# Second block's attention scores: the keys' low parts stored once per half, or twice, one below the other

## The chip, the cores and the metric

One NeuronCore of one Trainium2 chip runs the whole program. The metric is device time in microseconds (us) of that core. Engines are named as in the profile: PE (TensorE, matmuls), PEld (its weight loads), DVE (VectorE), ACT (ScalarE), POOL (GpSimd), SP (SyncE, which issues most DMAs).

## The reference

A transformer in float32 for 512 tokens of width 1024. A first block (hybrid mixer and a mixture of 32 experts) is followed by a second block of two equal layers. Each layer of the second block does, in short:

```python
h = rms_norm_2(x, norm_g); proj = h @ w_in          # split into q, k, v, z, gates
# stick-breaking attention, 8 heads of 64: scores, then a product of (1 - sigmoid) from the right
z = einsum('bhqd,bhkd->bhqk', qb, kb) * 64**-0.5    # by query blocks of 128, keys 0..end
o_a = w(z) @ vb
# sparse attention (nsa): 8 query heads share 2 key heads; compressed keys, selected keys, a window
ss = einsum('bgrqd,bgqkd->bgrqk', qb, ks) * scale   # selected: with 512 tokens all blocks up to the query
sw = einsum('bgrqd,bgkd->bgrqk', qb, kw) * scale    # window of 512
x = x + (sigmoid(ga)*(y_a @ w_up_a) + sigmoid(gb)*(y_b @ w_up_b)) @ w_out
```

Products of matrices are to be accurate to float32, so the kernel splits each operand into a high part (rounded to fp32r, the type that PE multiplies fast) and a low part, the rest, and adds the products that matter.

## The kernel before, in words

**Products.** A projection runs three matmuls for each of eight 128-row chunks: high x high, low x high, high x low (`rows_mm`, L371 to L373, 256 columns; `cols_mm`, L396 to L398, 512 columns). Each matmul has its own weight load, also where two in a row have the same stationary operand (L371 and L372).

**Scores.** A head has 64 channels, so the two parts of a query fill the 128 rows of one operand: `q_stack` (L405) puts the high part of head h in its 64 rows and the low part in the other 64. `k_stack` (L421) makes `kh`, which has the high part of the keys in both halves, with two ACT copies from PSUM (L428) and two DVE copies from SBUF (L434), and writes the low part once, to the head's own 64 rows of `kl` (DVE, L430). One `kl` tile holds the low parts of the two `k_stack` calls that belong together. `qk` (L437) then makes one score tile of 128 queries by 128, 256, 384 or 512 keys with two matmuls into the same PSUM bank: L442 over 128 rows gives (high + low query) x high key, and L443 over 64 rows gives high query x low key.

**Where scores are used.** `stick_attention` (L1713) calls `qk` 32 times a layer, four for each head. `nsa_weights` (L1976) calls it 64 times a layer: four query blocks, two key groups, two branches, four heads. That is 192 calls over the two layers, 48 of each width. The stick weights go through ACT (tanh, L1728), DVE (L1732, L1733), a scan along the keys (L1737) into one of two buffers `sbs`, and a subtraction that reads the scan (L1739). The nsa weights go through a mask and a maximum on DVE (L459, L461), an exponential on ACT (L464), and DVE again.

**Order.** Within a layer `weave` (L1651) mixes strands of work by estimated costs: the first part of the stick attention with the projections of its second half; the rest of it with the nsa projections and the compression network (`compress`); the nsa attention (L1949) with the large gate and up projections. The framework then places the instructions on the engines, and its order on each engine is fixed in the program: each engine runs its own list in order and waits where an operand or a buffer isn't ready.

**Buffers.** Most tiles of the second block, of up to 4 KB a partition, come from one pool, `hd`, of `NHD` = 17; a new tile waits until one is free. Smaller ones come from `P` (11). `sbs` has two buffers, the table of `gain_tables` (`rtab`, used by `rope_tile`) has one of its own, and so has `nf`, in which `nsa_finish` (L2021) makes the final sum.

Of the kernel before, what the change touches and what calls it, by code (L numbers as in the profile page):

```python
# [13 lines left out]
F32R = mybir.dt.float32r  # L14
I32 = mybir.dt.int32
BF16 = mybir.dt.bfloat16
AF = mybir.ActivationFunctionType
OP = mybir.AluOpType
AXX = mybir.AxisListType.X

P = 128
S = 512
NT = S // P
# [57 lines left out]
def rev(ap):  # L81
    a = [list(x) for x in ap.ap]
    s, n = a[-1]
    return bass.AP(tensor=ap.tensor, offset=ap.offset + s * (n - 1), ap=a[:-1] + [[-s, n]])


class Kern:
# [9 lines left out]


    NW, NWS = 2, 3
    KACT = False  # L100

    def run(self):
        with self.early():
            self.consts()
            with self.phase("first", NW2=1, NHT=17, NHD=8, NP=8):
                x = self.first_mixer()
            with self.phase("moe", NW2=4, NP=1):
                x, aT, late = self.moe(x)
        with self.phase("second", NW2=0, NHD=17, NP=11):
            self.second_block(x, aT, late)  # L110

    def early(self):
# [305 lines left out]
                                               op0=OP.mult, op1=OP.subtract)  # L418
        return q

    def k_stack(self, pt, kl):  # L421


        nc = self.nc
        kh = self.t([P, 2, S], F32R, tag="hd", bufs=self.NHD)
        rows = (slice(0, 64), slice(64, 128))
        for h in range(2):
            nc.scalar.activation(kh[rows[h], h, :], pt[rows[h], :], AF.Copy)  # L428
        for h in range(2):
            nc.vector.tensor_tensor(kl[rows[h], :], pt[rows[h], :], kh[rows[h], h, :], op=OP.subtract)  # L430
            if self.KACT:
                nc.scalar.copy(kh[rows[1 - h], h, :], kh[rows[h], h, :])
            else:
                nc.vector.tensor_copy(kh[rows[1 - h], h, :], kh[rows[h], h, :])  # L434
        return kh

    def qk(self, q, h, ts, k, n, out):  # L437

        nc = self.nc
        kh, kl = k  # L440
        r = slice(64 * h, 64 * h + 64)
        nc.tensor.matmul(out[:, :n], q[:, h, ts], kh[:, h, :n], start=True, stop=False)  # L442
        nc.tensor.matmul(out[:, :n], q[r, h, ts], kl[r, :n], start=False, stop=True)  # L443

    def transpose_rows(self, rows, f0, out, scale=None):

# [1176 lines left out]
    def gain_tables(self, gains):  # L1623

        nc = self.nc
        out = self.t([P, len(gains), 4, NT, 32], tag="rtab", bufs=1)
        for b, g in enumerate(gains):
            for n, (tab, half) in enumerate(((self.cos, 0), (self.sin, 1), (self.cos, 1), (self.sin, 0))):
                nc.gpsimd.tensor_tensor(out[:, b, n], tab, g[:, None, 32 * half:32 * half + 32].to_broadcast([P, NT, 32]),
                                        op=OP.mult)  # L1630
        return out
# [59 lines left out]

    def stick_qkz(self, l, aT, n, out):
        nc, W = self.nc, self.A["w_in_2"]
        kl = []

        def cons_q(m, ps):
            out[0, m] = self.q_stack(ps, 64 ** -0.5)

        def cons_k(m, ps):
            if not m:  # L1700
                kl.append(self.t([P, 2, S], F32R, tag="hd", bufs=self.NHD))
            out[2, m] = self.k_stack(ps, kl[0][:, m, :]), kl[0][:, m, :]

        def cons_z(m, ps):
            if not m:
                out[6] = self.hd_pair()
            o = out[6][:, m, :]
            nc.scalar.activation(o, ps, AF.Tanh, scale=0.5)
            nc.vector.scalar_tensor_tensor(o, o, 1.0, ps, op0=OP.add, op1=OP.mult)
        for base, cons in ((0, cons_q), (2, cons_k), (6, cons_z)):  # L1710
            yield from self.cols_steps(aT, W[l, base + n], cons)

    def stick_attention(self, qkz, v, y):  # L1713

        nc = self.nc

        def weights(h):

            c = h // 2
            q, k = (qkz[c // 2][base, c % 2] for base in (0, 2))  # L1720
            big, small = self.t([P, 1024], tag="hd", bufs=self.NHD), self.t([P, S], tag="P", bufs=self.NP)
            ws = [big[:, 896:1024], small[:, 0:256], big[:, 512:896], big[:, 0:512]]
            for i, w in enumerate(ws):
                n_ = (i + 1) * P
                sp = self.psum("s")
                self.qk(q, h % 2, slice(i * P, (i + 1) * P), k, n_, sp)
                f = self.t([P, S], tag="P", bufs=self.NP)
                nc.scalar.activation(f[:, :n_], sp[:, :n_], AF.Tanh, scale=0.5)  # L1728
                if i in self.SACT:
                    nc.scalar.activation(f[:, :n_], f[:, :n_], AF.Copy, scale=-0.5, bias=0.5)  # L1730
                else:
                    nc.vector.tensor_scalar(f[:, :n_], f[:, :n_], -0.5, 0.5, op0=OP.mult, op1=OP.add)  # L1732
                nc.vector.tensor_tensor(f[:, n_ - P:n_], f[:, n_ - P:n_], self.C["smask"], op=OP.max)  # L1733
                self.sbr = 1 - self.sbr
                sc = self.sbs[self.sbr]
                o = S - n_
                nc.vector.tensor_tensor_scan(rev(sc[:, o:S]), rev(f[:, :n_]),  # L1737
                                             self.zero.to_broadcast([P, n_]), 1.0, op0=OP.mult, op1=OP.add)
                nc.vector.tensor_tensor(w, sc[:, o + 1:], sc[:, o:S], op=OP.subtract)  # L1739
            return ws  # L1740

        ws = weights(0)
        yield 2.1
        for h in range(8):
            nxt = weights(h + 1) if h < 7 else None
            yield 2.1
            if h % 2 == 0:
                po = self.psum("o")
            r = slice(64 * (h % 2), 64 * (h % 2) + 64)
            for j in range(NT):  # L1750
                pt = self.psum("tr")
                for i in range(j, NT):
                    nc.tensor.transpose(pt[:, i * P:(i + 1) * P], ws[i][:, j * P:(j + 1) * P], self.ident)
                wT = self.t([P, S], tag="P", bufs=self.NP)
                nc.scalar.copy(wT[:, j * P:], pt[:, j * P:])
                nc.tensor.matmul(po[r, j * P:], v[h // 4][:, j, (h % 4) * 64:(h % 4 + 1) * 64], wT[:, j * P:],
                                 start=(j == 0), stop=(j == NT - 1), skip_group_check=True)
            ws = nxt
            if h % 2:
                c = h // 2  # L1760
                f = self.t([P, S], tag="P", bufs=self.NP)
                nc.vector.scalar_tensor_tensor(f, qkz[c // 2][6][:, c % 2, :], 0.5, po, op0=OP.mult, op1=OP.mult)
                nc.scalar.activation(y[0][:, c, :], f, AF.Copy)
                nc.vector.tensor_tensor(y[1][:, c, :], f, y[0][:, c, :], op=OP.subtract)
            yield 3.2
# [126 lines left out]
    def nsa_projections(self, l, aT, N):  # L1892
        nc, A, W = self.nc, self.A, self.A["w_in_2"]
# [11 lines left out]
                N["q"].append(self.q_stack(pt))  # L1905

        def k_stacks(rows):
            kl = self.t([P, 2, S], F32R, tag="hd", bufs=self.NHD)
            for n in range(2):
                pt = self.psum("tr")  # L1910
                self.transposes(rows, n * P, pt)
                N["k"].append((self.k_stack(pt, kl[:, n, :]), kl[:, n, :]))

        N["k"], N["q"] = [], []
        late = None
        for src, gains, dst in ((11, gk, k_stacks), (8, [gq], q_stacks), (9, None, q_stacks)):
            r = self.hd()
# [9 lines left out]
        v = N["v"] = [self.t([P, 2, 4, 2, 64], F32R, tag="hd", bufs=self.NHD) for _ in range(2)]  # L1927
# [93 lines left out]
    def nsa_finish(self, N, i, g, po):  # L2021

        nc = self.nc
        ts = slice(i * P, (i + 1) * P)
        cs = slice(2 * g, 2 * g + 2)
        f = self.t([P, 2, P], tag="nf", bufs=1)
        p4 = po.rearrange("p (c m q) -> p m c q", c=2, m=2)
        u = self.t([P, 2, 2, P], tag="P", bufs=self.NP)
        nc.scalar.copy(u[64:128], p4[64:128])
        for m in range(2):  # L2030
            nc.vector.tensor_tensor(f[64 * m:64 * m + 64], p4[0:64, m], u[64:128, m], op=OP.add)
        nc.vector.scalar_tensor_tensor(f, f, 0.5, N["z"][g][:, :, ts], op0=OP.mult, op1=OP.mult)
        if "y" not in N:
            N["y"] = self.split_y()
        yh, yl = N["y"]
        self.split(f, yh[:, cs, ts], yl[:, cs, ts])
# [131 lines left out]
    def second_block(self, x0, hl, late):  # L2168
        nc = self.nc
# [3 lines left out]
        self.fold = self.t([P, 64], tag="fold", bufs=1)  # L2173
        nc.vector.tensor_tensor(self.fold, self.ident[:, 0:64], self.ident[:, 64:128], op=OP.add)

        self.sbs, self.sbr = [self.t([P, S + 1], tag=f"sbs{n}", bufs=1) for n in range(2)], 0
        for sc in self.sbs:
            nc.vector.memset(sc[:, S:], 1.0)
        self.rope_tables()
        xo = self.O["out"].rearrange("(t p) d -> t p d", p=P)  # L2180
        x1 = self.x_in_dram(1)
# [147 lines left out]
```

## Time and profile before

| what | value |
|---|---|
| time, median of 3 runs | 2686.78 us (2685.45 to 2688.61) |
| the profiled execution's own time | 2686.94 us |
| its span (first to last instruction) | 2685.1 us |
| PE busy | 2561.9 us (95%) |
| DVE busy | 1796.4 us (67%) |
| ACT busy | 1275.6 us (48%) |

Busy shares are averages over stages with different limits: a stage is read from the windows. Matmuls overlap in the records (one may start before the one before it has ended), so what a matmul takes from PE is read from the distance between the starts of neighbours, not from its duration. The second block runs from about 1640 us to the end; its second layer repeats the first some 548 us later.

### The profile page before, as it was taken

The page shows a single profiled execution, that of the slowest core. Times are in us where ns is not written, and L with a number is a line of the kernel's source. Part 1 is how long each engine was busy: PE and PEld are TensorE (multiplying, and loading weights), DVE is VectorE, ACT ScalarE, POOL GpSimd, SP SyncE. Part 2 cuts the span into 40 slices and gives each one's busy share as a digit, 9 for nine tenths or more (in the row PEclk, how much of TensorE's full clock was granted, in tenths as well). Part 3 has the DMA queues.
Part 4 walks back from the last instruction along what each step waited for, and adds up shares of the span by engine and source line. Part 5 has one row for each costly group of instructions (what it writes and reads, how often), then busy time and mean ns, then how long its engine had stood idle before and what let it go on. Part 6 is the DMA issues. An engine that isn't in the chain of part 4 may idle for free.

```text
span 2685.1 us, 40235 instructions
## 1 busy us (share of the span) xinstructions
PE 2561.9 (95%) x15431; PEld 2003.9 (75%) x15431; DVE 1796.4 (67%) x3400; ACT 1275.6 (48%) x2202; POOL 159.9 (6%) x151
## 2 busy tenths in 40 slices
PE   5998879999999999999999969989999999999998
PEld 5875678777777778777777757776777887767778
DVE  6886667666666688666666645596775656877764
ACT  3443546545555566444455534444444433534443
POOL 1001010100000000000000010011001000100001
PEclk9998788999999999999999989999999999999999
DMA  7531236999699999999999952221112521311124
GB/s 283 203 120 65 77 134 254 367 376 367 228 359 376 380 363 344 383 379 376 380 376 384 378 192 79 67 93 66 46 48 79 189 95 49 111 63 48 33 84 151
DMA packets 85828, 566.77 MB, mean 211 GB/s; under 512 B 9984, under 2 KB 10576, under 8 KB 22144
## 3 DMA queue, kind: packets, MB, share of 16 engines
q1 hardware_dynamic: 76368, 536.55, 51.5%
q0 software_dynamic: 7968, 24.16, 3.9%
q10 hardware_dynamic: 1296, 3.44, 0.3%
q8 instruction: 123, 2.02, 0.3%
q14 instruction: 73, 0.60, 0.1%
HBM read 543.93 MB, written 20.19 MB: 210 GB/s over the span
## 4 chain that ended last, share of the span: by engine, by line
PE 72%; DVE 6%; DMA 2%; ACT 2%; issue 2%; POOL 1%; ACTq 0%; DVEq 0%; SPq 0%; POOLq 0%
PE mm L396 5%; PE mm L397 5%; PE mm L398 5%; PE mm L1290 4%; PE s L1290 4%; PE o L1290 4%; PE o L1278 3%; PE mm L1276 3%; PE mm L1278 2%; PE o L1276 2%; PE o L1277 2%; PE s L1276 2%; PE mm L1277 2%; PE s L1278 2%; PE s L1277 2%; PE o L1192 2%
## 5 line engine op out<-in xcount | busy, mean ns | idle before, releaser
L1260 ACT ACTIVATE wh<-w 128x1024 fp32r<-128x1024 f32 x324 | 337.5, 1060 | 286.2 <-DMA w<-w_exp 131.7
L1261 DVE TENSOR_TENSOR wl<-w,wh 128x1024 fp32r<-128x1024 f32 x324 | 388.2, 1221 | 84.8 <-ACT wh L1260 84.0
L215 DVE TENSOR_TENSOR wl<-w,wh 128x1024 fp32r<-128x1024 f32 x194 | 237.0, 1223 | 176.3 <-ACT wh L214 175.1
L214 ACT ACTIVATE wh<-w 128x1024 fp32r<-128x1024 f32 x194 | 204.8, 1059 | 234.6 <-PE mm L397 97.9
L372 PE MATMUL mm<-wl,aTh 128*128 128x256 f32 x816 | 238.1, 293 | 5.6 <-DVE wl L215 5.6
L371 PE MATMUL mm<-wh,aTh 128*128 128x256 f32 x816 | 238.7, 294 | 2.2 <-ACT wh L214 1.3
L373 PE MATMUL mm<-wh,aTl 128*128 128x256 f32 x816 | 238.1, 293 | 0.8 <-DVE aTl L309 0.8
L396 PE MATMUL mm<-aTh,wh 128*128 128x512 f32 x560 | 228.3, 408 | 0.0
L397 PE MATMUL mm<-aTl,wh 128*128 128x512 f32 x560 | 225.5, 403 | 0.0
L398 PE MATMUL mm<-aTh,wl 128*128 128x512 f32 x560 | 224.9, 402 | 0.0
L372 PEld LDWEIGHTS mm<-wl,aTh 128*128 128x128 f32 x816 | 161.0, 197 | 9.4 <-DVE wl L215 6.3
L371 PEld LDWEIGHTS mm<-wh,aTh 128*128 128x128 f32 x816 | 160.4, 197 | 6.6 <-ACT wh L214 1.9
L373 PEld LDWEIGHTS mm<-wh,aTl 128*128 128x128 f32 x816 | 160.7, 197 | 4.5 <-issue 3.1
L464 ACT ACTIVATE P<-s,smx 128x256 f32<-128x256 f32 (+3 forms) x176 | 92.7, 528 | 86.8 <-DVE smx L461 85.7
L1261 DVE TENSOR_TENSOR spl<-w,sph 128x1024 fp32r<-128x1024 f32 x108 | 132.1, 1223 | 1.2 <-ACT sph L1260 1.2
L1260 ACT ACTIVATE sph<-w 128x1024 fp32r<-128x1024 f32 x108 | 114.2, 1057 | 26.5 <-PE mm L1277 10.3
L396 PEld LDWEIGHTS mm<-aTh,wh 128*128 128x128 f32 x560 | 106.3, 190 | 24.1 <-issue 4.9
L398 PEld LDWEIGHTS mm<-aTh,wl 128*128 128x128 f32 x560 | 106.3, 190 | 23.8 <-issue 3.0
L397 PEld LDWEIGHTS mm<-aTl,wh 128*128 128x128 f32 x560 | 105.8, 189 | 23.2 <-issue 3.8
L1319 DVE TENSOR_SCALAR eg<-s 128x512 f32<-128x512 f32 (+1 forms) x66 | 37.6, 569 | 111.6 <-PE s L1280 71.6
L1290 PE MATMUL mm<-w,xN 128*64 128x256 f32 x960 | 110.2, 382 | 0.0
L1290 PE MATMUL s<-w,xN 128*64 128x256 f32 x960 | 109.5, 381 | 0.0
(617 smaller groups left out, 6073.7 us busy)
## 6 DMA issues: line engine op xcount, KB each, us to landing
w<-w_exp SPq DMA_DIRECT2D x384, 1024.0 KB, 8.9
w<-w_in SPq DMA_DIRECT2D x57, 1024.0 KB, 4.8
w<-w_out SPq DMA_DIRECT2D x24, 1024.0 KB, 4.9
w<-ada_w SPq DMA_DIRECT2D x19, 1024.0 KB, 4.9
w<-cmp_w SPq DMA_DIRECT2D x8, 1024.0 KB, 4.8
w<-w_up SPq DMA_DIRECT2D x16, 512.0 KB, 3.3
xm<-hd POOLq DMA_DIRECT2D x5, 512.0 KB, 3.6
aTl<-ada_w SPq DMA_DIRECT2D x2, 1024.0 KB, 7.8
```

Of the source, the lines that this page charges most:

```text
L214: self.nc.scalar.activation(hi, src, AF.Copy)
L215: (self.nc.gpsimd if pool else self.nc.vector).tensor_tensor(lo, src, hi, op=OP.subtract)
L371: nc.tensor.matmul(v[:, q, :], ah[k][:, ts], w_h, start=(k == 0), stop=False)
L372: nc.tensor.matmul(v[:, q, :], ah[k][:, ts], w_l, start=False, stop=False)
L373: nc.tensor.matmul(v[:, q, :], al[k][:, ts], w_h, start=False, stop=(k == kk - 1))
L396: nc.tensor.matmul(ps, w_h, ah[k], start=(k == 0), stop=False)
L397: nc.tensor.matmul(ps, w_h, al[k], start=False, stop=False)
L398: nc.tensor.matmul(ps, w_l, ah[k], start=False, stop=(k == kk - 1))
L1260: nc.scalar.activation(hi, w, AF.Copy)
L1261: (nc.gpsimd if n in self.LO_POOL else nc.vector).tensor_tensor(lo, w, hi, op=OP.subtract)
L1276: nc.tensor.matmul(ps, xh[:, k, :], wh[:, q, :], start=(k == 0), stop=False)
L1290: nc.tensor.matmul(ps[CN * c:CN * (c + 1), 0:256], a, w[:, c * 256:(c + 1) * 256], start=(n == 0), stop=(n == len(jobs) - 1))
```

## The change

The low parts get the form of the high parts. `k_stack` now allocates a `kl` tile of its own, of the size of `kh`, and writes the low part of each head to both halves, so that `qk` runs both matmuls over 128 rows with the same stationary operand; the product low query x low key is added to the score by that. All copies of the high part are now made by ACT from PSUM, and all four low parts by DVE from PSUM.

```diff
-        with self.phase("second", NW2=0, NHD=17, NP=11):
+        with self.phase("second", NW2=0, NHD=19, NP=11):
...
-    def k_stack(self, pt, kl):
+    def k_stack(self, pt):
...
-        kh = self.t([P, 2, S], F32R, tag="hd", bufs=self.NHD)
+        kh, kl = (self.t([P, 2, S], F32R, tag="hd", bufs=self.NHD) for _ in range(2))
         rows = (slice(0, 64), slice(64, 128))
         for h in range(2):
-            nc.scalar.activation(kh[rows[h], h, :], pt[rows[h], :], AF.Copy)
+            for r in (h, 1 - h):
+                nc.scalar.activation(kh[rows[r], h, :], pt[rows[h], :], AF.Copy)
         for h in range(2):
-            nc.vector.tensor_tensor(kl[rows[h], :], pt[rows[h], :], kh[rows[h], h, :], op=OP.subtract)
-            if self.KACT:
-                nc.scalar.copy(kh[rows[1 - h], h, :], kh[rows[h], h, :])
-            else:
-                nc.vector.tensor_copy(kh[rows[1 - h], h, :], kh[rows[h], h, :])
-        return kh
+            for r in (h, 1 - h):
+                nc.vector.tensor_tensor(kl[rows[r], h, :], pt[rows[h], :], kh[rows[h], h, :], op=OP.subtract)
+        return kh, kl
...
-        kh, kl = k
-        r = slice(64 * h, 64 * h + 64)
-        nc.tensor.matmul(out[:, :n], q[:, h, ts], kh[:, h, :n], start=True, stop=False)
-        nc.tensor.matmul(out[:, :n], q[r, h, ts], kl[r, :n], start=False, stop=True)
+        for m, v in enumerate(k):
+            self.nc.tensor.matmul(out[:, :n], q[:, h, ts], v[:, h, :n], start=(m == 0), stop=(m == 1))
...
-        out = self.t([P, len(gains), 4, NT, 32], tag="rtab", bufs=1)
+        out = self.t([P, len(gains), 4, NT, 32], tag="hd", bufs=self.NHD)
...
-                self.sbr = 1 - self.sbr
-                sc = self.sbs[self.sbr]
+                sc = self.sbs
...
-        f = self.t([P, 2, P], tag="nf", bufs=1)
+        f = self.t([P, 2, P], tag="P", bufs=self.NP)
...
-        self.sbs, self.sbr = [self.t([P, S + 1], tag=f"sbs{n}", bufs=1) for n in range(2)], 0
-        for sc in self.sbs:
-            nc.vector.memset(sc[:, S:], 1.0)
+        self.sbs = self.t([P, S + 1], tag="sbs", bufs=1)
+        nc.vector.memset(self.sbs[:, S:], 1.0)
```

The callers (`stick_qkz`, L1692, and `k_stacks` in `nsa_projections`, L1907) lose the shared `kl` tile that they made. The scan has one buffer, and the rope tables and the final sum of the nsa attention move to the pools `hd` (two buffers more) and `P` (as many as before).

## Rows read from the trace of the kernel before

**Rows 1.** The page's head: the span, and PE's busy time and share.
```profile
span 2685.1 us, 40235 instructions
PE 2561.9 (95%) x15431; PEld 2003.9 (75%) x15431; DVE 1796.4 (67%) x3400; ACT 1275.6 (48%) x2202; POOL 159.9 (6%) x151
```

**Rows 2.** Windows, first layer of the second block: busy us of each engine (instructions).
```profile
core 0: us, PE busy (x) PEld busy (x) DVE busy (x) ACT busy (x) POOL busy (x), PEclk, DMA share, GB/s
1640.00:1740.00 100.00, 99.28 (x511) 73.73 (x510) 63.27 (x120) 40.67 (x79) 0.71 (x2) 1.00 0.17 62
1740.00:1840.00 100.00, 92.38 (x575) 74.20 (x574) 87.48 (x188) 46.57 (x82) 18.26 (x25) 0.98 0.26 88
1840.00:2050.00 210.00, 209.31 (x984) 150.84 (x983) 149.98 (x388) 103.94 (x241) 1.08 (x2) 1.00 0.15 53
```

**Rows 3.** The same windows, instructions of L443 alone.
```profile
1640.00:1740.00 100.00, 8.20 (x20) 3.66 (x20) 1.00 0.17 62
1740.00:1840.00 100.00, 5.20 (x12) 2.30 (x12) 0.98 0.26 88
1840.00:2050.00 210.00, 26.21 (x64) 11.70 (x64) 1.00 0.15 53
```

**Rows 4.** Timeline of PE, a 512-column score (start us, duration us, instruction).
```profile
1857.26 0.39 PE L398 MATMUL mm<-yh,wl 128*128 128x512 f32 x1
1857.49 0.40 PE L442 MATMUL s<-hd,hd 128*128 128x512 f32 x1
1857.82 0.50 PE L443 MATMUL s<-hd,hd 64*128 64x512 f32 x1
1858.25 0.50 PE L396 MATMUL mm<-yh,wh 128*128 128x512 f32 x1
```

**Rows 5.** Timeline of PEld around it: weight loads, idle before them.
```profile
1857.27 0.19 PEld L442 LDWEIGHTS s<-hd,hd 128*128 128x128 f32 x1
1857.82 0.18 PEld L443 LDWEIGHTS s<-hd,hd 64*128 64x128 f32 x1 [0.36 <-issue]
```

**Rows 6.** Timeline of PE, a 384-column score.
```profile
1938.70 0.39 PE L397 MATMUL mm<-aTl,wh 128*128 128x512 f32 x1
1938.93 0.33 PE L442 MATMUL s<-hd,hd 128*128 128x384 f32 x1
1939.19 0.44 PE L443 MATMUL s<-hd,hd 64*128 64x384 f32 x1
1939.56 0.50 PE L398 MATMUL mm<-aTh,wl 128*128 128x512 f32 x1
```

**Rows 7.** Timeline of PE, a 128-column and a 256-column score.
```profile
1723.08 0.28 PE L373 MATMUL mm<-wh,aTl 128*128 128x256 f32 x1
1723.20 0.22 PE L442 MATMUL s<-hd,hd 128*128 128x128 f32 x1
1723.35 0.32 PE L443 MATMUL s<-hd,hd 64*128 64x128 f32 x1
1723.60 0.38 PE L442 MATMUL s<-hd,hd 128*128 128x256 f32 x1
1723.91 0.38 PE L443 MATMUL s<-hd,hd 64*128 64x256 f32 x1
1724.22 0.39 PE L371 MATMUL mm<-wh,aTh 128*128 128x256 f32 x1
```

**Rows 8.** Timeline of PE: sixteen short matmuls in a row, each with a full weight load.
```profile
1915.30 1.86 PE L2046 MATMUL s<-ckT,hd 128*128 128x32 f32 x16
```

**Rows 9.** Groups by line and shape from 1600 us on: `k_stack`'s instructions.
```profile
L430 DVE TENSOR_TENSOR hd<-mm,hd 64x512 fp32r<-64x512 f32 x16 | 11.0, 689 | 0.6 <-ACT hd L428 0.4
L434 DVE CAST hd<-hd 64x512 fp32r<-64x512 f32 x24 | 10.1, 422 | 5.7 <-ACT hd L428 5.1
L428 ACT ACTIVATE hd<-mm 64x512 fp32r<-64x512 f32 x16 | 9.5, 592 | 14.4 <-PE mm L398 14.2
```

**Rows 10.** Timeline of DVE: two scans, and the two subtractions that read them.
```profile
1803.90 2.07 DVE L1737 TENSOR_TENSOR_SCAN sbs<-P,zero 128x384 f32<-128x384 f32 x2
1805.88 1.13 DVE L1739 TENSOR_TENSOR hd<-sbs 128x384 f32<-128x384 f32 x2
```

**Rows 11.** Waits of POOL, 1600 to 1840 us: total us, times, longest.
```profile
POOL hd L1794 <- PE s L443: 20.4, 1, 20.4
```

More of the change, by code (lines that the diff above doesn't have):

```diff
@@ L99 @@
     NW, NWS = 2, 3
-    KACT = False
     def run(self):
@@ L419, in q_stack @@
         return q
-    def k_stack(self, pt, kl):
+    def k_stack(self, pt):
         nc = self.nc
-        kh = self.t([P, 2, S], F32R, tag="hd", bufs=self.NHD)
+        kh, kl = (self.t([P, 2, S], F32R, tag="hd", bufs=self.NHD) for _ in range(2))
         rows = (slice(0, 64), slice(64, 128))
         for h in range(2):
-            nc.scalar.activation(kh[rows[h], h, :], pt[rows[h], :], AF.Copy)
+            for r in (h, 1 - h):
+                nc.scalar.activation(kh[rows[r], h, :], pt[rows[h], :], AF.Copy)
         for h in range(2):
-            nc.vector.tensor_tensor(kl[rows[h], :], pt[rows[h], :], kh[rows[h], h, :], op=OP.subtract)
-            if self.KACT:
-                nc.scalar.copy(kh[rows[1 - h], h, :], kh[rows[h], h, :])
-            else:
-                nc.vector.tensor_copy(kh[rows[1 - h], h, :], kh[rows[h], h, :])
-        return kh
-    def qk(self, q, h, ts, k, n, out):
-        nc = self.nc
-        kh, kl = k
-        r = slice(64 * h, 64 * h + 64)
-        nc.tensor.matmul(out[:, :n], q[:, h, ts], kh[:, h, :n], start=True, stop=False)
-        nc.tensor.matmul(out[:, :n], q[r, h, ts], kl[r, :n], start=False, stop=True)
+            for r in (h, 1 - h):
+                nc.vector.tensor_tensor(kl[rows[r], h, :], pt[rows[h], :], kh[rows[h], h, :], op=OP.subtract)
+        return kh, kl
+    def qk(self, q, h, ts, k, n, out):
+        for m, v in enumerate(k):
+            self.nc.tensor.matmul(out[:, :n], q[:, h, ts], v[:, h, :n], start=(m == 0), stop=(m == 1))
     def transpose_rows(self, rows, f0, out, scale=None):
@@ L1693, in stick_qkz @@
         nc, W = self.nc, self.A["w_in_2"]
-        kl = []
         def cons_q(m, ps):
@@ L1699, in cons_k @@
         def cons_k(m, ps):
-            if not m:
-                kl.append(self.t([P, 2, S], F32R, tag="hd", bufs=self.NHD))
-            out[2, m] = self.k_stack(ps, kl[0][:, m, :]), kl[0][:, m, :]
+            out[2, m] = self.k_stack(ps)
         def cons_z(m, ps):
@@ L1907, in k_stacks @@
         def k_stacks(rows):
-            kl = self.t([P, 2, S], F32R, tag="hd", bufs=self.NHD)
             for n in range(2):
@@ L1911, in k_stacks @@
                 self.transposes(rows, n * P, pt)
-                N["k"].append((self.k_stack(pt, kl[:, n, :]), kl[:, n, :]))
+                N["k"].append(self.k_stack(pt))
         N["k"], N["q"] = [], []
```

## The prediction, made before the run

> **What bounds the kernel now.** I read the page's head first: PE is busy for 95% of the span [rows 1], so time that PE does not have to spend is worth looking for. An average hides stages, so the windows of the second block came next [rows 2]. The reader is to see three kinds. From 1640 to 1740 us (stick attention beside projections) PE is busy 99.28 of 100 us and DVE 63.27. From 1840 to 2050 us (nsa attention beside gate and up projections) PE has 209.31 of 210, DVE 149.98. Between them, 1740 to 1840 us, PE has 92.38 and DVE 87.48: there both are close to full and waits on DVE show. Third, the same windows for L443 alone [rows 3] place the matmul that changes: 20, 12 and 64 of it; the second layer has the same counts 548 us later. So 168 of the 192 lie where PE sets the pace, and 24 in the mixed stretch. Last, the timeline of PE, where I compare starts, because recorded durations overlap.
>
> **The two score matmuls.** A 512-column matmul between its like follows the one before it by 0.23 us: L442 starts 0.23 after L398 [rows 4]. Then the rhythm breaks: L443 starts 0.33 after L442, and the next full-height matmul 0.43 after L443. The weight load shows why: L443's begins only at 1857.82, with its matmul, after 0.36 us of idle PEld that nothing released ("issue"), where L442's load began 0.22 ahead of its own [rows 5]. So a load for 64 rows doesn't slip under a running 128-row matmul, nor one for 128 rows under a 64-row matmul; PE pays at entry and at exit. After the change no row count alternates, so I price each pair by the rhythm of full-height matmuls.
>
> By start differences, from the matmul ahead of the pair to the one behind it:
> - 512 columns: 1858.25 - 1857.26 = 0.99 against 3 x 0.23 = 0.69: 0.30 lost [rows 4].
> - 384: 1939.56 - 1938.70 = 0.86 [rows 6] against 0.23 + 2 x 0.18 = 0.59 (0.18 lies between 0.23 for 512 and 0.12 for 256): 0.27.
> - 128 and 256 together: 1724.22 - 1723.08 = 1.14 for five matmuls [rows 7]. A 256-column one costs 0.12 (L373 to L442). A 128-column one can't go below a full weight load: sixteen in 1.86 us, 0.12 each [rows 8]. So 5 x 0.12 = 0.60 against 1.14: 0.54 for two pairs, 0.27 each.
>
> These rows are typical of the 48 pairs of each width, but a lone 128-column pair has least to lose, as its streaming is short and the weight loads, 0.12 each, stay; so I take 0.27 as the mean. Terms: 168 x 0.27 = 45 us in the stretches that PE bounds. In the mixed stretches 24 x 0.27 = 6.5; half of it counts where PE and DVE take turns in holding the end: 3.
>
> The bounds: nothing (if the rhythm stays broken) and 192 x 0.30 = 58 us.
>
> The Trainium skill, "TensorEngine Tiling (Array Packing)", Key Properties, says that a change of tiling mode drains the engine; the gaps above agree with it [rows 4, 5]. The Trainium skill, "TensorE: Matmul & The Clock Gate", section on packing small matmuls, says that a weight load overlaps running matmuls only where its row group differs, which speaks against this change; by it the sum would be zero. This trace disagrees with that as a general rule: L442's load, on the same 128 rows, ran under L398 [rows 5]. The same page of the Trainium skill, in Part 2's step on LDWEIGHTS, allows a load into a background buffer.
>
> **`k_stack`.** Twelve calls, six a layer. DVE: two SBUF copies of 0.42 become two PSUM subtractions of 0.69 [rows 9], so 2 x 0.27 = 0.53 a call, 6.4 us in all. Eight calls (stick) lie where DVE has a third free: nothing, and 4.3 us if that cover went. Four (nsa) lie in the mixed stretches, with DVE at 87%: +2 us in full. ACT: two more copies of 0.59 a call, 14 us in all, on an engine with 47 of 100 us busy in its fullest stretch [rows 2]: nothing; what is queued behind them on ACT is the next split of weights or a tanh, late by 1.2 us once a call, at most 14 us if nothing hid it. The `mm` bank is held about 1 us longer (four subtractions behind the first copy, not three DVE operations); PE fills the other bank for some 5 us (24 x 0.23) meanwhile, so it doesn't wait.
>
> **One scan buffer.** Scan and subtraction are both on DVE, in order, so no engine waits; what goes is the freedom to put two scans ahead of two subtractions. Those four took from 1803.90 to 1807.01, 3.11 us, against 2.07 + 1.13 = 3.20 laid end to end [rows 10]: overlap of 0.09 a hand-over. For 64 scans at most 64 x 0.09 = 6 us of DVE; in the mixed stretches about 1 us counts. One memset fewer: nothing.
>
> **Pools.** `hd` grows by 2; live tiles grow by one `kl` for each pair of `k_stack` calls and one or two tables. The pool already ran dry once a layer, when POOL's memset of L1794 waited 20.4 us for the last reader of a stick key tile, L443 [rows 11], unseen by PE. But the separate `kl` of the first two heads is also free earlier than the shared one. I take zero, bounds in the rivals. `f` in `P`, eight times a layer, lives for under a few DVE operations: zero. More `hd` tiles may also let row loads go earlier; they aren't late now: zero.
>
> **What is late next.** In the nsa stretch PE's work shrinks by 64 x 0.27 = 17 of 210 us; DVE's share rises from 149.98/210 = 71% to 150/193 = 78%. The chain score, mask, maximum, exponential, scaling has less time beside the woven matmuls, and some waits will show. I take 10% of the 35 us of both layers: +3.
>
> **Sum.** -45 - 3 + 2 + 1 + 3 = -42 us, on the profiled execution's own 2686.9 us (span 2685.1 and 1.8 around it), which is the median of the runs to 0.2 us: 2645 us.
>
> **The rivals.**
> - A, all of it comes through: 0.30 on all 192 pairs, nothing given back: 58 us, 2629. For: chains of pairs, as in the stick heads, lose more than lone ones. Against: DVE at 87% in the mixed stretches.
> - B, half is given back: the nsa chain or the fuller `hd` pool becomes the limit where PE now has work to spare: -21, 2666. For: DVE reaches three quarters of the time there, and latencies of four hand-overs a score don't shrink. Against: today's 209.31 of 210 shows that the woven work fills the gaps with ease.
> - C, the rhythm stays broken, because the price lies with something other than the row count (the two matmuls of one bank, or the same operand loaded twice): then only the added work remains, +3: 2690. By the Trainium skill's overlap rule (above) it would come out this way too. Against: L371 and L372 load one operand twice at 0.12 each, and L442's early load.
> - D, slower: `hd` runs dry on a tile whose writer is ACT or DVE and not POOL. Up to four more tiles are live against two more buffers (a third `kl`, two tables). If in each layer two waits like the 20.4 us of L1794 stood in ACT's queue, where the splits that feed PE lie, that is 4 x 20.4 = 82 us: 2645 + 82 = 2727. It decides from 21 us of such waits a layer (42 / 2). Against: the first such wait falls on POOL, and two of the `kl` tiles are freed earlier.
>
> **How the numbers follow.** Forecast 57%, with its own range 2634 to 2656 (0.23 to 0.30 a pair, give-back 0 to 6); A 17%, B 18%, C 4%, D 4%. About 0.2%, 5.4 us, is what a measurement of this kernel tells from no change; C lies within it. Faster 0.92, same 0.04, slower 0.04. The range takes in the forecast, most of A and B: 2627 to 2670.
>
> **What would show it.** In the changed profile the second score matmul has 128 rows; the next matmul starts 0.23 us after it for 512 columns, 0.12 for 256; PEld shows no "issue" idle before its load. The nsa windows shrink by about 16 us a layer, the first stick window by 5 to 6, the mixed one by 1 or less. Wrong: starts 0.4 us apart as now (C); the nsa window shorter by under 10 us with waits on DVE before PE's transposes (B); an idle ACT or DVE before a write to `hd`, released by L443 or its successor (D).

## The result, and the profile after

The changed kernel takes 2646.76 us (median of 4 runs, 2645.29 to 2652.6) against 2686.11 us of the kernel before: a ratio of 0.9857, 95% interval 0.984 to 0.9874. The forecast was 2645 us. The profiled execution has a span of 2643.4 us, 41.7 less than before.

The page's head of the changed kernel, beside [rows 1]: PE is busy 57 us less in all, its share of the span is the same.
```profile
span 2643.4 us, 40269 instructions
PE 2505.1 (95%) x15431; PEld 1991.4 (75%) x15431; DVE 1803.3 (68%) x3399; ACT 1287.9 (49%) x2226; POOL 157.6 (6%) x151
```

PE's timeline at the same 512-column score as in [rows 4] (two matmuls of one line and one name stand in one row, x2), then its weight loads, as in [rows 5]:
```profile
1852.44 0.39 PE L397 MATMUL mm<-yh,wl 128*128 128x512 f32 x1
1852.67 0.62 PE L438 MATMUL s<-hd,hd 128*128 128x512 f32 x2
1853.13 0.39 PE L395 MATMUL mm<-yh,wh 128*128 128x512 f32 x1
```
```profile
1852.44 0.42 PEld L438 LDWEIGHTS s<-hd,hd 128*128 128x128 f32 x2
1852.90 0.19 PEld L395 LDWEIGHTS mm<-yh,wh 128*128 128x128 f32 x1
```
From the matmul ahead to the one behind, 1853.13 - 1852.44 = 0.69 us, where it was 0.99: the rhythm of 3 x 0.23 to the hundredth. Both loads of the pair start while a matmul runs, and the "issue" idle is gone here. (Before, it stood on both sides of the 64-row matmul. This is the load of the full-height matmul behind it, the row that follows [rows 5]:)
```profile
1858.25 0.19 PEld L396 LDWEIGHTS mm<-yh,wh 128*128 128x128 f32 x1 [0.25 <-issue]
```
For 256 columns, which lost about 0.27 a pair before:
```profile
1701.38 0.39 PE L397 MATMUL mm<-aTh,P 128*24 128x512 f32 x1
1701.61 0.40 PE L438 MATMUL s<-hd,hd 128*128 128x256 f32 x2
1701.85 0.28 PE L370 MATMUL mm<-wh,aTh 128*128 128x256 f32 x1
```
Here 1701.85 - 1701.38 = 0.47 = 0.23 + 2 x 0.12.

The windows of [rows 2 and 3], moved so that they hold the same work (40, 24 and 128 of the new L438, two a score): busy us of PE, PEld, DVE, ACT, POOL, then L438 alone.
```profile
1637.50:1735.50 98.00, 93.57 (x513) 72.95 (x512) 66.59 (x120) 43.29 (x85) 7.16 (x14) 1.00 0.19 66
1735.50:1835.50 100.00, 88.94 (x571) 73.54 (x570) 87.72 (x188) 48.82 (x86) 10.76 (x13) 0.98 0.25 87
1835.50:2028.00 192.50, 191.69 (x987) 148.41 (x987) 149.62 (x388) 103.59 (x241) 1.08 (x2) 1.00 0.17 58
```
```profile
1637.50:1735.50 98.00, 8.76 (x40) 6.41 (x40) 1.00 0.19 66
1735.50:1835.50 100.00, 5.93 (x24) 3.77 (x24) 0.98 0.25 87
1835.50:2028.00 192.50, 32.99 (x128) 21.21 (x128) 1.00 0.17 58
```
The nsa window is 17.5 us shorter, with PE still busy to the last 0.8 us and DVE at 149.62 of 192.5, 78%. The first stick window is only 2 us shorter: PE is idle there for 4.4 us, where it was for 0.7, and for 11 us in the mixed one, where it was for 7.6.

What PE waited for (total us, times, longest), the largest rows, from 1640 to 1840 us before, and in the same stretch after, 1637.5 to 1835.5 us:
```profile
PE mm L372 <- DVE wl L215: 2.5, 1, 2.5
PE s L1811 <- DVE hd L215: 1.9, 2, 1.6
PE tr L1753 <- DVE hd L430: 0.8, 1, 0.8
PE tr L1753 <- DVE hd L415: 0.8, 2, 0.5
```
```profile
PE s L1802 <- DVE hd L214: 4.3, 2, 3.5
PE tr L1744 <- DVE hd L431: 2.3, 2, 1.8
PE tr L1744 <- DVE hd L414: 2.0, 2, 1.2
PE tr L1810 <- DVE chu L1814: 1.5, 1, 1.5
```
(L1802 is the compression network's matmul, L1811 before; L1744 the transposes of stick weights, L1753 before; L214 splits an operand into its high and low part, L215 before; L431 is `k_stack`'s subtraction, L414 the one of `q_stack`.) In these rows DVE's work is late for PE. In the first stick window alone, 1637.5 to 1735.5 us, the longest row is ACT's tanh (L1720), and one wait is on `k_stack`:
```profile
PE s L438 <- ACT P L1720: 1.3, 3, 0.6
PE s L1802 <- DVE hd L214: 0.9, 1, 0.9
PE mm L397 <- DVE P L214: 0.8, 1, 0.8
PE mm L395 <- DVE hd L431: 0.5, 1, 0.5
```

The table of stages, worked out from start times in the two traces: a stage runs between the first copy of a layer's `stick_v`, its last stick tanh, its last scaling of nsa weights and the next layer's first copy.

| stage | before, us | after, us | difference |
|---|---|---|---|
| up to the second block | 1597.5 | 1595.1 | -2.4 |
| layer 1, projections and stick | 228.6 | 226.4 | -2.2 |
| layer 1, nsa | 216.2 | 198.6 | -17.6 |
| rest of layer 1 | 98.6 | 99.2 | +0.6 |
| layer 2, projections and stick | 233.2 | 229.0 | -4.2 |
| layer 2, nsa | 216.3 | 198.6 | -17.7 |
| rest | 94.7 | 96.5 | +1.8 |

The first row isn't the change's: that work is the same, and its length varied between 1592.8 and 1599.2 us over the profiled runs. A difference of a few us between two profiled executions is therefore read from the stages behind it.

### The profile page after: what moved, and what is told of

Its sections match the earlier page's. It is cut to its first block, busy times and chain, and to the rows that moved or that the text cites. A ratio compares the mean times of both kernels' runs of the same rounds, so it can differ in the third digit from the quotient of the medians.

```text
span 2643.4 us, 40269 instructions
## 1 busy us (share of the span) xinstructions
PE 2505.1 (95%) x15431; PEld 1991.4 (75%) x15431; DVE 1803.3 (68%) x3399; ACT 1287.9 (49%) x2226; POOL 157.6 (6%) x151
## 4 chain that ended last, share of the span: by engine, by line
PE 67%; DVE 9%; DMA 3%; ACT 3%; issue 2%; POOL 1%; ACTq 0%; DVEq 0%; SPq 0%; POOLq 0%
PE mm L395 5%; PE mm L397 5%; PE mm L396 4%; PE mm L1285 4%; PE s L1285 4%; PE o L1285 4%; PE o L1273 3%; PE mm L1271 3%; PE mm L1273 2%; PE o L1271 2%; PE mm L1272 2%; PE o L1272 2%; PE o L1187 2%; PE s L1271 2%; PE s L1273 2%; PE s L1272 2%
## 5 line engine op out<-in xcount | busy, mean ns | idle before, releaser
L214 DVE TENSOR_TENSOR wl<-w,wh 128x1024 fp32r<-128x1024 f32 x194 | 237.3, 1226 | 154.4 <-ACT wh L213 152.7
```

Source lines behind the costliest of these rows:

```text
L214: (self.nc.gpsimd if pool else self.nc.vector).tensor_tensor(lo, src, hi, op=OP.subtract)
```

## The experiments

All times are medians; ratios are to the kernel before, run on the same chip at the same time (2685.65 to 2687.0 us).

| run | us | ratio | 95% interval |
|---|---|---|---|
| changed kernel | 2646.76 | 0.9857 | 0.984 to 0.9874 |
| second matmul over 64 rows (e1) | 2692.33 | 1.0021 | 1.0011 to 1.0031 |
| both over 64 rows (e3) | 2685.31 | 0.9993 | 0.9984 to 1.0003 |
| 64 rows in stick alone (e4) | 2657.39 | 0.9893 | 0.9876 to 0.9911 |
| 64 rows in nsa alone (e5) | 2681.52 | 0.998 | 0.9971 to 0.999 |
| pools alone (e2) | 2687.92 | 1.0 | 0.9991 to 1.0009 |
| low copy from SBUF by DVE (e9) | 2641.38 | 0.9831 | 0.9817 to 0.9844 |
| e1 and e9 together (e10) | 2686.92 | 1.0001 | 0.9992 to 1.001 |
| low copy by POOL (e8) | 2639.62 | 0.9823 | 0.981 to 0.9836 |
| two scan buffers, 18 hd (e6) | 2651.79 | 0.987 | 0.9855 to 0.9885 |
| 18 hd (e7) | 2645.11 | 0.9843 | 0.983 to 0.9857 |
| a third full-height matmul (e11) | 2683.66 | 0.9986 | 0.9977 to 0.9995 |

**Undo the row count alone (e1).**
```diff
-        for m, v in enumerate(k):
-            self.nc.tensor.matmul(out[:, :n], q[:, h, ts], v[:, h, :n], start=(m == 0), stop=(m == 1))
+        r = slice(64 * h, 64 * h + 64)
+        self.nc.tensor.matmul(out[:, :n], q[:, h, ts], k[0][:, h, :n], start=True, stop=False)
+        self.nc.tensor.matmul(out[:, :n], q[r, h, ts], k[1][r, h, :n], start=False, stop=True)
```


> The changed kernel, but the second score matmul runs over the head's own 64 rows again (of q and of the doubled kl); k_stack, pools and the order of every engine's instructions stay. Leaves out low query x low key, as the kernel before did. Theory (a change of row count between neighbouring matmuls costs PE about 0.27 us a pair, where PE sets the pace): +40 to +50 us, 2687 to 2697, that is the time of before and a few us for the added DVE work. Rival (the gain came from the larger pool and the new order): no change, 2647. Rival (half and half): 2667.

Measured: 2692.33, 45.6 above the changed kernel. The broken rhythm is back in its timeline, 1860.38 - 1859.40 = 0.98 us:
```profile
1859.40 0.39 PE L397 MATMUL mm<-yh,wl 128*128 128x512 f32 x1
1859.63 0.39 PE L437 MATMUL s<-hd,hd 128*128 128x512 f32 x1
1859.95 0.50 PE L438 MATMUL s<-hd,hd 64*128 64x512 f32 x1
1860.38 0.50 PE L395 MATMUL mm<-yh,wh 128*128 128x512 f32 x1
```
In the trace each engine runs its instructions in the changed kernel's order, so the rivals of pool and order fall. It is also 6.5 us above the time of before (interval 3 to 8), so something in the rest of the change costs time.

**Both over 64 rows (e3).**
```diff
+        r = slice(64 * h, 64 * h + 64)
         for m, v in enumerate(k):
-            self.nc.tensor.matmul(out[:, :n], q[:, h, ts], v[:, h, :n], start=(m == 0), stop=(m == 1))
+            self.nc.tensor.matmul(out[:, :n], q[r, h, ts], v[r, h, :n], start=(m == 0), stop=(m == 1))
```


> The changed kernel with both score matmuls over the head's own 64 rows; order unchanged. Leaves out low query x high key and low x low. Theory (price per change of row count: one entry and one exit a pair, nothing between the two): the time of the run with one 64-row matmul, 2687 to 2697. Rival (price per 64-row matmul, whatever stands beside it): twice the loss, about 2735. Rival (a weight load cannot hide under a matmul on the same rows, so equal neighbours pay too): above 2697 as well, but then the changed kernel itself would not have gained.

Measured: 2685.31, not twice the loss. PE's and PEld's timelines at the same score:
```profile
1852.36 0.40 PE L397 MATMUL mm<-yh,wl 128*128 128x512 f32 x1
1852.69 0.73 PE L438 MATMUL s<-hd,hd 64*128 64x512 f32 x2
1853.35 0.50 PE L395 MATMUL mm<-yh,wh 128*128 128x512 f32 x1
```
```profile
1852.69 0.29 PEld L438 LDWEIGHTS s<-hd,hd 64*128 64x128 f32 x2 [0.37 <-issue]
1853.35 0.19 PEld L395 LDWEIGHTS mm<-yh,wh 128*128 128x128 f32 x1 [0.37 <-issue]
```
The pair takes 1853.35 - 1852.36 = 0.99 us, as with one of 64 rows, but the two loads run together in 0.29 us with no idle between them, and PEld stands still (0.37) only ahead of the first and behind the second. So the price is per change of row count, not per 64-row matmul, and a load does hide under a matmul on the same rows. The Trainium skill, "TensorEngine Tiling (Array Packing)", Key Properties, says that a change of tiling mode drains the engine; a price per change agrees with that.

That this run is 7 us under e1 was not forecast, but the traces show where it comes from. Its nsa stretches are as long as e1's (215.7 twice against 215.9), its stick stretches 3.2 and 3.0 us shorter. In nsa nearly every pair stands alone between full-height matmuls; in stick two pairs of one head, on the same 64 rows, mostly stand directly behind each other. Such a chain changes the row count four times in e1 and twice in e3. The same chain, 128 and 256 columns, by the matmuls ahead of it and behind it: in e1 (as in [rows 7]), in e3 (with its four matmuls), in the changed kernel:
```profile
1724.26 0.28 PE L372 MATMUL mm<-wh,aTl 128*128 128x256 f32 x1
1725.41 0.39 PE L370 MATMUL mm<-wh,aTh 128*128 128x256 f32 x1
```
```profile
1717.83 0.28 PE L372 MATMUL mm<-wh,aTl 128*128 128x256 f32 x1
1718.04 0.72 PE L438 MATMUL s<-hd,hd 64*128 64x128 f32 x4
1718.68 0.39 PE L370 MATMUL mm<-wh,aTh 128*128 128x256 f32 x1
```
```profile
1718.76 0.28 PE L372 MATMUL mm<-wh,aTl 128*128 128x256 f32 x1
1719.34 0.28 PE L370 MATMUL mm<-wh,aTh 128*128 128x256 f32 x1
```
That is 1.15, 0.85 and 0.58 us: four changes, two, and none.

**Where the pairs stand: stick (e4) and nsa (e5) alone.**
```diff
-    def qk(self, q, h, ts, k, n, out):
+    def qk(self, q, h, ts, k, n, out, low64=False):
         for m, v in enumerate(k):
-            self.nc.tensor.matmul(out[:, :n], q[:, h, ts], v[:, h, :n], start=(m == 0), stop=(m == 1))
+            r = slice(64 * h, 64 * h + 64) if m and low64 else slice(0, P)
+            self.nc.tensor.matmul(out[:, :n], q[r, h, ts], v[r, h, :n], start=(m == 0), stop=(m == 1))
...
# e4: low64=True in stick_attention's call; e5: in nsa_weights' call
```


> The changed kernel with the 64-row second matmul in the 64 stick calls alone; order unchanged. By the prediction's terms (40 pairs at 0.27 and 24 at half of it): +14 us, 2661. By the landmarks of the two traces, in which the stick stretches became only some 2 and 4 us shorter: +6, 2653.

> The changed kernel with the 64-row second matmul in the 128 nsa calls alone; order unchanged. By the prediction's terms, 128 x 0.27 = 35 less the give-back of 3: +32, 2679. By the landmarks (17.6 and 17.7 us a layer): +35, 2682. If the nsa stretch were bound by the softmax chain: +17 or less, 2664.

Measured: e4 10.6 us above the changed kernel, e5 34.8; together 45.4, e1's 45.6. By stages, e4's stick stretches are 5.4 and 5.9 us longer with nsa unchanged (198.5 twice), e5's nsa stretches 17.3 and 17.4. So nsa gives back nothing: 34.8 / 128 = 0.27 us a pair. Stick gives 10.6 / 64 = 0.17, between its two forecasts. The stage table's stick gain (2.2 + 4.2 = 6.4) is smaller still: some 4 us of added cost stand beside the pairs there. The first stick window and the mixed one of e4, moved so that they hold the work of the changed kernel's:
```profile
1638.15:1740.50 102.35, 100.14 (x513) 73.86 (x512) 66.62 (x120) 43.55 (x85) 7.16 (x14) 1.00 0.18 63
1740.50:1841.50 101.00, 94.75 (x571) 77.00 (x570) 87.73 (x188) 48.88 (x86) 10.78 (x13) 0.95 0.24 86
```
They are 4.35 and 1.0 us longer than the changed kernel's 98 and 100: 20 pairs at 0.22 and 12 at 0.08 (in the second layer, by start times, 4.3 and 1.6). PE is idle for 2.2 and 6.3 us here and for 4.4 and 11.1 in the changed kernel, with the same `k_stack` and the same order on every engine: shorter pairs in stick end in part in longer waits, 7 us of them in the first layer. The mean granted clock is 1.00 in the first window of both, 0.95 against 0.98 in the mixed one, and 1.00 in the nsa windows.

**The pools alone on the kernel before (e2).**
```diff
-        with self.phase("second", NW2=0, NHD=17, NP=11):
+        with self.phase("second", NW2=0, NHD=19, NP=11):
...
# and: rtab in hd, nf in P, one scan buffer, as in the change
```


> The kernel before (old k_stack, old score matmuls) with the change's pools alone: 19 hd buffers, rope tables in hd, the final sum in P, one scan buffer. Theory (pools are worth nothing, the one scan buffer about +1): 2686 to 2688. Rival (the pools, by waits or by the order that they bring, are the 6.5 us that the undone row count is above the time of before): 2692. Rival (the larger pool is itself a gain): below 2680.

Measured: a ratio of 1.0, 0.9991 to 1.0009, which is 2.4 us either way. The pools with the single scan buffer don't explain the 6.5 us; what is left is `k_stack`, with ACT's copies and the order that came with it.

**The second low part copied from SBUF (e9), and with 64 rows (e10).**
```diff
-            for r in (h, 1 - h):
-                nc.vector.tensor_tensor(kl[rows[r], h, :], pt[rows[h], :], kh[rows[h], h, :], op=OP.subtract)
+            nc.vector.tensor_tensor(kl[rows[h], h, :], pt[rows[h], :], kh[rows[h], h, :], op=OP.subtract)
+            nc.vector.tensor_copy(kl[rows[1 - h], h, :], kl[rows[h], h, :])
```


> The changed kernel, but DVE makes the second copy of the low part from the first one in SBUF (0.42 us by the copies of the kernel before) and not by a second subtraction from PSUM (0.69 us): 6.4 us less DVE work, 2 us of it in the mixed stretches. By the prediction's term: -2 us, 2645. Rival (DVE's work is hidden there too): no change, 2647. Rival (k_stack's added DVE work is all of the 6.5 us): -6, 2641.

> Two edits on the changed kernel: the second matmul over 64 rows again, and the second copy of the low part made by DVE from SBUF. Leaves out low query x low key. What stood 6.5 us above the time of before with the 64-row matmul alone was, if it is k_stack's second subtraction, gone by 5.4 us: 2687, and the row count is worth the same 45 us in this order (2641 + 45 = 2686). If the 6.5 us is the pools' or ACT's copies: 2692.

Measured: e9 2641.38, 5.4 under the changed kernel (the intervals overlap a little); e10 2686.92, 5.4 under e1 and just clear of it, and equal to the kernel before. e10 has as much DVE work in `k_stack` as before, the new ACT copies and the new pools, so the latter two cost nothing that shows, and the second subtraction from PSUM costs 5.4 in place of the copy from SBUF. But this isn't DVE's 6.4 us alone: with the shorter copy the framework also chose another order (against the changed kernel, some 110 of PE's instructions and 45 of DVE's in the second block stand at other places), and no run holds the order and changes the copy. How much of the 5.4 is the work and how much the order is not shown.

e9 and e10 have one order on every engine, and differ by the row count alone: 45.5 us, as e1 showed in the other order (45.6). PE's waits from 1637.5 to 1835.5 us in e9:
```profile
PE tr L1744 <- DVE hd L430: 2.1, 1, 2.1
PE tr L1810 <- DVE chu L1814: 1.9, 1, 1.9
PE tr L1744 <- DVE hd L414: 1.4, 2, 0.9
PE s L1802 <- DVE hd L214: 0.9, 1, 0.9
```
The wait of the compression matmul on its split, 4.3 us in the changed kernel, is 0.9 here; the others change by 0.6 at most.

**The copy on POOL (e8).**
```diff
-            for r in (h, 1 - h):
-                nc.vector.tensor_tensor(kl[rows[r], h, :], pt[rows[h], :], kh[rows[h], h, :], op=OP.subtract)
+            nc.vector.tensor_tensor(kl[rows[h], h, :], pt[rows[h], :], kh[rows[h], h, :], op=OP.subtract)
+            nc.gpsimd.tensor_copy(kl[rows[1 - h], h, :], kl[rows[h], h, :])
```


> The changed kernel, but the second copy of the low part is made by POOL from the first one in SBUF, not by DVE from PSUM: 24 fewer subtractions of 0.69 us on DVE, 16.5 us, of which 5.5 us in the stretches where DVE is fullest. Theory (DVE's added work costs what falls in the mixed stretches): -3 to -5 us, 2643. Rival (POOL, slower and busy with the rope there, is late for the scores): +3 or more, 2650.

Measured: 2639.62, 7.1 under the changed kernel and clear of it, more than the 3 to 5 expected, and the lowest of all runs; 1.8 from e9, which the intervals don't tell apart. The order changed here too. POOL's copies took 0.70 us each:
```profile
L431 POOL CAST hd<-hd 64x512 fp32r<-64x512 f32 x24 | 16.8, 701 | 246.8 <-DVE hd L430 219.1 <-DVE rsy L236 12.1 <-issue 12.1
```

**Two scan buffers (e6), 18 hd buffers (e7).**
```diff
-        with self.phase("second", NW2=0, NHD=19, NP=11):
+        with self.phase("second", NW2=0, NHD=18, NP=11):
...
# e6 alone: two sbs buffers used in turn, as before the change
```


> The changed kernel with two scan buffers again; hd has 18 buffers to make room (the order of all engines is that of 19). By the prediction's term for the scan buffer: -1 us, 2646. If the one buffer is what holds the stick stretches: -4 or more, 2643. If the nineteenth hd buffer matters: above 2650.

> The changed kernel with 18 hd buffers, one less; the order of all engines is the same. Tells the two edits of the run with two scan buffers (2652) apart. If the nineteenth buffer is worth 5 us: 2652. If it is the freedom of the second scan buffer, which lets a later scan go ahead of a subtraction, that costs: 2647.

Measured: e7 2645.11, the changed kernel's time in the changed kernel's order; e6 2651.79, 6.7 above e7, with each of its runs above each of e7's. The nineteenth buffer is worth nothing that shows. The second scan buffer brings another order (on DVE some scans, the line L1737 of before, go ahead of the subtraction that stood before them), but its cost is less sure than the medians look: of the 7.1 us between the two profiled executions 4.7 stand before the second block, where the work is the same. Behind it the stick stretches are 1.4 and 5.1 us longer (the second layer's 233.9 against 228.8), the other stages together 4.1 shorter. The second layer's stick windows of e6 and e7:
```profile
2123.00:2357.00 234.00, 219.86 (x1296) 181.22 (x1297) 164.32 (x318) 105.10 (x189) 19.51 (x25) 0.97 0.23 80
2118.00:2347.00 229.00, 212.77 (x1292) 175.23 (x1291) 164.63 (x316) 104.65 (x189) 18.62 (x25) 1.00 0.23 83
```
PE is idle for 14.1 us in e6 and for 16.2 in e7, but busy 7 us longer, at a mean granted clock of 0.97 against 1.00: here the longer time is busy time at the lower clock, not waits on DVE. Why the clock was lower in e6 was not tried.

**A third full-height matmul (e11).**
```diff
-        for m, v in enumerate(k):
-            self.nc.tensor.matmul(out[:, :n], q[:, h, ts], v[:, h, :n], start=(m == 0), stop=(m == 1))
+        for m, v in enumerate((k[0], k[1], k[1])):
+            self.nc.tensor.matmul(out[:, :n], q[:, h, ts], v[:, h, :n], start=(m == 0), stop=(m == 2))
```


> The changed kernel with a third full-height matmul in each score (the low part added twice): 48 x (0.12 + 0.12 + 0.18 + 0.23) = 31 us more of PE at the rhythm of full-height matmuls. Theory (PE sets the pace and full-height neighbours cost only their rhythm): +28 to +33, 2677. If the woven stretches had slack: +15 or less. If a load could not hide under a matmul on the same rows: +60 or more. The order of the engines shifts a little, so some us either way say nothing.

Measured: 36.9 above the changed kernel, some 6 over the rhythm's 31 and above the range expected; the order shifted too. By stages, stick is 6.4 and 10.8 us longer, nsa and the rest of a layer together 10.0 and 9.8, about 64 x 0.16. So added PE time costs its full price. That a shorter pair pays in full doesn't follow: e4 shows that it doesn't in stick.

## Why the prediction was right, and by which steps

- **The pairs.** The mechanism held: full-height neighbours keep 0.23 and 0.12 us. Foretold 45 + 3 = 48 us for all 192; with the order held, e1 measured 45.6. The split was a little off: nsa 34.8 (35 foretold), stick with the mixed stretch 10.6 (14). The mixed windows came out as foretold (1.0 and 1.6 us, 1.6 foretold); the first stick windows gave 4.3 each, not 5.4.
- **Give-back.** Foretold 3, in the nsa chain; none is seen there (17.6 and 17.7 us of 17 a layer, PE idle 0.8 us). B falls: DVE at 78% was enough. The give-back stood in the stick stretches, outside the mixed window too, where the prediction had none: PE's waits there grew as the pairs became shorter (e4).
- **`k_stack`.** The mis-sized term. "Nothing" for the eight stick calls "where DVE has a third free" was wrong. Foretold +2; measured 5.4, for the second subtraction with the order that it brings (e10 against e1). The place shows in e4, whose stick pairs have 64 rows as before: its stick stretches are 3.2 and 1.7 us longer than before (231.8 and 234.9 against 228.6 and 233.2), and of the 3.2 us 2.4 stand in the first stick window (102.35 us against 100), where DVE is the least busy. The step on the `mm` bank ("so it doesn't wait") failed too, by little: a projection waits 0.5 us a layer for L431, by the code for the bank that L431 reads. The nsa calls read a `tr` bank, which the prediction didn't look at, and there the transposes wait 2.3 us, where it was 0.8 (the waits of 1637.5 to 1835.5 us). These waits alone are not the 5.4: the one on the `tr` bank is still 2.1 in e9. The cover that was named existed in the window, not at the place.
- **One scan buffer.** Foretold +1, which e2's 2.4 us either way can't tell from nothing. Two buffers in the new kernel are no gain (e6 against e7). What they cost, and whether by order or by the clock, is open.
- **Pools and ACT's copies.** Zero foretold, none seen (e2, e7, e10). D falls; `hd` with 18 is as good.
- **C** falls: the rhythm is whole again (0.69 us), and e1 breaks it by the row count alone. With it falls, as a general rule, the one of the Trainium skill, "TensorE: Matmul & The Clock Gate", section on packing small matmuls, that a weight load overlaps running matmuls only where its row group differs: in the changed kernel both loads of a pair run under matmuls on the same 128 rows, in e3 on the same 64.

One of the signs that were named missed: the first stick window shrank by 2 us, not by 5 to 6. Its pairs gave 4.3, and `k_stack` with its order took 2.4 back.

That the sum came out, 39.4 us of gain by medians against 42, is in part luck. Stick's pairs gave 3.4 us less and `k_stack` cost 3.4 more than foretold; on the other side stand 3 us of give-back that didn't come in nsa and the 1 us of the scan buffer that isn't seen. The 35 us of the nsa pairs, most of the sum, are no luck.

## What to carry to other kernels

Look at the distance between starts where matmuls of different row counts alternate: here each such pair lost about 0.27 us where PE set the pace. No wait row of PE names it; it stands with PEld, as "issue", in `before` on 140 of the 192 loads:
```profile
PEld s L443 <- issue: 35.5, 140, 0.4
```
Filling the rows with a second copy bought it back for 0.4 to 0.7 us of copying a head, and each copy serves four scores in stick and 16 in nsa. Ask what PE waits for next behind the copy: an engine that is a third idle on average is not off the path, and the same copy on POOL, or from SBUF, was worth 5 to 7 us here, with the order that came along. When nothing but one edit is to be priced, hold the order of instructions: e4 and e5 then added up to e1 within 0.2 us.

## What the runs showed that was not expected

Two 64-row matmuls on the same rows overlap their loads as full-height ones do (0.29 us for both, no idle): only the change of row count stops PEld, for 0.37 us on either side in e3. So two 64-row pairs behind each other share one entry and one exit (0.85 us where e1 took 1.15). In stick, shorter pairs made PE wait longer for DVE and ACT, though the order and all other work were the same. And a second buffer for the scan, which takes a dependence away, made nothing faster: 2651.79 against 2645.11 us, with 4.7 us of the profiled difference in work that the buffer doesn't touch, and a lower granted clock in the second layer's stick stretch.
